# Norm rows stored unsplit, scaled rows in their own tiles, one gate product on another engine

## The chip, the cores and the metric

The kernel runs on one core of a Trainium2 chip. The metric is the time of one execution on the device in microseconds (us), the median of several runs. In the profile PE is TensorE (PEld its weight loads), DVE is VectorE, ACT is ScalarE, POOL is GpSimd and SP is SyncE, which here issues nearly all DMAs.

## The reference, cut to what matters

One layer of a diffusion backbone over 2048 latent tokens of width 1024 with a context of 256 tokens, all in float32. Two groups of heads (a gated recurrence in both directions and a spatial gating unit, "sgu") read one input projection. Around the change it computes:

```python
o_mlp = chunk_sgu(...)                       # gelu(u) * (W_s LN(gelu(v)) + b), per head and 128 positions
o = concatenate([o_hg, o_mlp], axis=-1)
x = x + g1 * (o @ w_out[l])                  # output projection, 1024 x 1024
h2 = modulate(rmsnorm(x, norm_ffn[l]), sh2, sc2)
...
a, g = split(h2 @ w_up[l], 2)                # up-projection, 1024 x 5632
x = x + g2 * ((a * gelu(conv3x3(g) + conv_b)) @ w_down[l])
return rmsnorm(x, norm_final)
```

## The kernel before

**Products.** A float32 matrix is used as a sum of two rounded parts, high and low: a copy on ScalarE rounds the high part, a subtraction gives the low part (`split`, lines 135 to 140). A product of two such pairs is three matmul passes (high by high, high by low, low by high). The output projection and the up-projection each multiply 2 x 2 blocks with seven block products in place of eight (Strassen's scheme in Winograd's form). The seven right-hand operands live in seven pairs of tiles `B[i]`, `B[i][0]` the high part, `B[i][1]` the low; `products` issues a product of 12 matmuls of 512 columns, on weights `Ah`, `Al`. `Unit.prep` makes these from `raw` rows: per product a cast on ScalarE and a subtraction on GpSimd (L140), and for four of the seven products a sum on GpSimd (L1247 to L1253). It runs three products ahead (`LOOK`). Products 2, 3, 5 and 6 add onto a bank of PSUM (`ux`, `uz`) that must first be read by the addition of an earlier product, on VectorE (L1378 in the output projection).

**Stages in order.** (1) The projection with the heads. The last head's sgu makes, for each of two 512-column parts (`n0` = 0 and 512), a layernorm (`ln`), four spatial matmuls and a scaling (`mix`, L717), and a product with gelu(u) on GpSimd (`both`, L685), whose result is stored to `oT_d`. At four banks before the end `open_wo` frees the heads' tiles and queues `load`, which fetches the first rows of `oT_d` and splits the first two operands of `w_out`. (2) The output projection: eight pairs of row tiles (`pairs`, n = 0 to 7), seven products each in the order 0, 1, 2, 4, 3, 6, 5 (`SEVEN`). Rows of x are fetched by `fetch_x` (L1350), the products added to them (L1378), the result stored to `xn_d` (L1388). (3) With it, the second norm, one pair behind: sum of squares on ScalarE (L1389), the root on GpSimd (`rstd`), scaling of the rows in place (L1300), then four steps `k` of four transposes each on PE (L1303), two activations that modulate (L1315) and three differences that make the seven operands (L1318 to L1320). The steps start a set stretch of modelled PE time after the pair's last product (`how`: 10.0, then every 2.6). For the first half (n = 0 to 3) they're stored as they are in `yd[0]` (L1322); for the second (n = 4 to 7) they are split into high and low, and both are stored in `yd[1]` (L1326, L1327). (4) The up-projection, first half then second: during pair 7 the first half's operands are loaded from `yd[0]` on ScalarE's DMA queue (L1391) and split in `B` (`in_place`). After an operand's last use in the first half its two parts for the second are loaded from `yd[1]` (`load_b`, L1409). Then the down-projection.

**What sets the order.** Each engine works through its own queue in order. A scheduler places instructions of a queue by a model of their readiness, except that those under `pin` keep their order in the program; `tc.issue_after(i)` puts what is inside it behind instruction `i` of its engine. Work at the side is queued in two pumps (`hg_q`, `bg_q`) and let in between matmuls by modelled PE time. DMAs issued by SP also go in the order of its queue: one that waits holds up those behind it.

**Tiles around the change.** `px` holds `cv` (3 tiles, rows of x), `fl` (2, the norm's seven operands), `yst` (2, their high part); `pv`, opened at block 4 in place of `po`, holds `v` (3, rows of x). `po` holds the first rows of the projection (`first0`, `first1`), two pairs of weights and a sum for row tile 0.

Of the kernel before, what the change touches and what calls it, by code (L numbers as in the profile page):

```python
# [9 lines left out]
F32 = mybir.dt.float32  # L10
# [8 lines left out]
P = 128  # L19
# [69 lines left out]
def tile_trunk(ctx, tc, x, c, cx, c_ctx, w_ada, b_ada, norm_mix, norm_ffn, w_in, hg_norm, sgu_g, sgu_b,  # L89
# [107 lines left out]
    with es1:  # L197
# [480 lines left out]
        def sgu(hh, h):  # L678
# [3 lines left out]
            def both(n0):  # L682
                if n0 in z and n0 in u:
                    zt = z.pop(n0)
                    G.tensor_mul(zt, zt, u.pop(n0))  # L685
                    st(oT_d[hh][:, 4 + h, n0:n0 + 512], zt)
# [6 lines left out]
            def sv(n0, n, pj):  # L693
# [3 lines left out]
                def ln():  # L697
# [217 lines left out]

        def in_place(i):
            split(B[i][0], B[i][1], B[i][1].bitcast(F32), V, pin)

# [218 lines left out]
        def open_wo():  # L1137
# [5 lines left out]
            po = eso.enter_context(tc.tile_pool(name="po", bufs=1, side="right", reuse_waits="tile"))  # L1143

            def load():
                ahead.extend(po.tile([P, 4, 2 * P], F32, name=f"first{k}") for k in range(2))
                ahead.extend(tuple(po.tile([P, 4, P], F32R, name=f"A{w}{i}", align_bytes=AL) for w in "hl") for i in range(2))
                ahead.append(po.tile([P, 4, P], F32, name="s2"))
                four = pw.tile([P, 4, 4, 512], F32R, name="four", align_bytes=AL)
                for n, (i, w) in enumerate(((1, 0), (2, 1), (2, 0), (4, 1))):  # L1150
                    B[i][w] = four[:, n]
# [122 lines left out]
    yd = [dr.tile([P, 2, 7, 4, 512], F32, name=f"yd{hh}") for hh in range(2)]  # L1274

# [17 lines left out]
    with ExitStack() as esv:  # L1293
        def second_norm(hh, g0, xs, ss, bank_, first, step):

            r = rstd(px, ss, 2, 1.0 / D)

            def scale():
                for i in range(2):
                    scaled.append(pin(V.tensor_scalar(out=xs[i], in0=xs[i], scalar1=r[:, i:i + 1], scalar2=None,  # L1300
                                                      op0=ALU.mult)))
            yield scale
            yield first  # L1303
            cl = slice(g0 // 2 * P, g0 // 2 * P + P)
            for k in range(4):
                pt = bank_()
                for kk in range(2):
                    for i in range(2):
                        o = kk * 256 + i * P
                        T.transpose(pt[:, o:o + P], xs[i][:, (k + 4 * kk) * P:(k + 4 * kk + 1) * P], ident)  # L1310
# [9 lines left out]
                V.tensor_sub(fl[:, 6, :], fl[:, 1, :], fl[:, 2, :])  # L1320
# [13 lines left out]
        def prep_o(m):  # L1334
# [8 lines left out]
            elif n == NCH - 1 and i in (6, 5):  # L1343
                units[1].load_half(6 - i)

        def fetch_x(n):
            out = []
            for i in range(2):
                t = v_tile()[:, :D] if i or n in (0, NCH - 1) else pv.tile([P, D], F32, tag="v", name="v", bufs=3)
                ld(t, x[(2 * n + i) * P:(2 * n + i + 1) * P, :])  # L1350
                out.append(t)
                if n == 0:
                    wo_raw((3, 6)[i])
            return out

        xts = {0: fetch_x(0)}
        wo_raw(5)
        pairs[1].load()
        in_place(4)
        with tc.issue_after(rooted[-1].ins):  # L1360
            for m in range(LOOK):
                prep_o(m)
        todo = {2: lambda: in_place(3), 3: lambda: in_place(6), 4: lambda: in_place(5)}
        later, scales = {}, {}
        for m, (u, i) in enumerate(blocks):
            n = pairs.index(u)
            if i == 0:
                u.x, xs = xbank(), xts.pop(n)
                ss = px.tile([P, 2], F32, tag="ss", name="ss", bufs=2)
                if 0 < n < NCH - 1:  # L1370
                    xts[n + 1] = fetch_x(n + 1)
            elif i == 4:
# [9 lines left out]
            prep_o(m + LOOK)  # L1382
            if m == 4:
                eso.close()
                pv = esv.enter_context(tc.tile_pool(name="pv", bufs=1, side="right", reuse_waits="tile"))
                xts[1] = fetch_x(1)
            if i in (6, 5):
                st(xn_d[2 * n + c], xs[c])  # L1388
                S.activation(dbank().rearrange("p a b -> p (a b)"), xs[c], AF.Square, accum_out=ss[:, c:c + 1])  # L1389
            if n == NCH - 1:  # L1390
                todo[m + 1] = lambda i=i: S.dma_start(B[i][1].bitcast(F32), yd[0][:, 0, i])  # L1391
                later[m + 4] = lambda i=i: in_place(i)
            if i == 5:
                how = (10.0, 2.6) if n + 1 < NCH else (10.0, 4.5)
                norm = second_norm(u.hh, u.f, xs, ss, lambda: dbank()[:, 0, :], *how)
                bg_q.drain()
# [9 lines left out]
    pf = esx.enter_context(tc.tile_pool(name="pf", bufs=1, reuse_waits="tile"))  # L1406

    def load_b(hh, i, w):
        ld(B[i][w].bitcast(F32), yd[hh][:, w, i])  # L1409

# [176 lines left out]
    for n, (u, i) in enumerate(prods):  # L1587
# [14 lines left out]
        if n == 12:  # L1602
            edges = px.tile([P, 7, P], F32R, tag="yst", name="edges", bufs=2).bitcast(F32)
            edges = edges[:, :4, :].rearrange("p f (w c) -> p f w c", w=2)
        with tc.issue_after(scaled[-1].ins) if n < 8 else nullcontext():
# [280 lines left out]
```

## Time and profile before

| | us |
|---|---|
| median of 3 runs | 2431.0 |
| lowest, highest | 2428.29, 2431.53 |
| the profiled execution | 2425.86 |
| its span, first to last instruction | 2423.8 |

The profiled execution has a mean granted TensorE clock of 0.988. Where rows of the profile are shown, a line of the timeline has the start, the duration, the engine, the line of the kernel, the operation, what it writes and reads, its shape and how many of them were merged; what stands in brackets is how long the engine was idle before it, and what ended that. A line of waits has the engine that waited, for whom, the sum in us, the number of times and the longest. A line of groups has the number of instructions, then busy us and mean ns of one, then the idle time before them.

The larger costs by name: `pj` is the input projection, `ux` and `uz` are the banks of the seven-product stages, `dn` is used by the norm's transposes, the convolution and the down-projection.

### The profile page before, as it was taken

What the parts mean: (1) busy time and instruction counts of PE and PEld (TensorE: products, weight loads), DVE (VectorE), ACT (ScalarE), POOL (GpSimd) and SP (SyncE); (2) the same over time, 40 slices, a digit from 0 to 9 for tenths busy, and PEclk for the clock granted to TensorE, in tenths of its full rate; (3) what the DMA queues carried; (4) which work ended last, traced back from release to release, by engine and by line L of the source; (5) the groups of instructions that cost most, each with busy time, mean ns of one, the idle gap of its engine ahead of it and who ended that gap; (6) DMA issues with size and microseconds to landing.
All of it is one profiled execution on the core that took longest, in us unless ns stands there. A gap on an engine that the chain in (4) does not pass through costs nothing.

```text
span 2423.8 us, 37053 instructions
## 1 busy us (share of the span) xinstructions
PE 2338.8 (96%) x14059; PEld 1923.4 (79%) x14059; DVE 1666.0 (69%) x2158; ACT 1058.3 (44%) x1820; POOL 1011.8 (42%) x875
## 2 busy tenths in 40 slices
PE   7999999999999998996899999999999999999998
PEld 6887878877887876775788888888888887888887
DVE  4767687576667666776896666549777763776876
ACT  3554443444455444445544444344444443332243
POOL 0022121111112327764887878878788860000002
PEclk8999999999999998998999999999999999999999
DMA  8465455664444226669322232642222238834645
GB/s 309 125 202 163 160 157 187 232 208 138 160 149 131 101 76 234 219 231 296 107 94 82 91 97 78 239 178 97 93 87 92 84 125 336 306 118 152 229 149 200
DMA packets 300695, 394.63 MB, mean 163 GB/s; under 512 B 32581, under 2 KB 219229, under 8 KB 296933
## 3 DMA queue, kind: packets, MB, share of 16 engines
q1 hardware_dynamic: 296220, 384.17, 47.0%
q10 hardware_dynamic: 4297, 8.10, 1.1%
q8 instruction: 110, 1.80, 0.3%
q14 instruction: 68, 0.56, 0.1%
HBM read 284.13 MB, written 108.08 MB: 162 GB/s over the span
## 4 chain that ended last, share of the span: by engine, by line
PE 46%; issue 2%; DMA 2%; POOL 1%; DVE 1%; ACT 0%; SPq 0%; POOLq 0%; DVEq 0%; ACTq 0%
PE ux L70 19%; PE uz L70 14%; PE dn L70 13%; DMA sT<-wd 1%; POOL rr L1746 1%; DMA sS<-m 0%; DMA mr<-m 0%; DMA yd<-yst 0%; DVE rest L140 0%; ACT four L139 0%; POOL raw L1251 0%; POOL ra L1745 0%; SPq L1671 0%; POOL Al L140 0%; POOL ra L1743 0%
## 5 line engine op out<-in xcount | busy, mean ns | idle before, releaser
L1453 DVE SCALAR_TENSOR_TENSOR dn<-gp,taps,dn 128x1024 f32<-128x1024 f32 x352 | 448.2, 1284 | 99.6 <-ACT dn L1450 95.0
L140 POOL TENSOR_TENSOR Al<-raw,Ah 128x512 fp32r<-128x512 f32 x306 | 404.7, 1338 | 100.0 <-ACT Ah L139 55.9
L70 PE MATMUL dn<-thl,mhl 128*128 128x512 f32 x1680 | 383.6, 390 | 3.4 <-ACT thl L139 3.2
L70 PEld LDWEIGHTS dn<-thl,mhl 128*128 128x128 f32 x1680 | 316.0, 188 | 70.9 <-ACT thl L139 4.1
L70 PE MATMUL pj<-xh,whi 128*128 128x512 f32 x896 | 366.4, 409 | 0.0
L70 PE MATMUL pj<-xl,whi 128*128 128x512 f32 x896 | 351.6, 393 | 0.0
L70 PE MATMUL pj<-xh,wlo 128*128 128x512 f32 x896 | 350.6, 392 | 0.0
L139 ACT CAST Ah<-raw 128x512 fp32r<-128x512 f32 x306 | 188.6, 619 | 270.9 <-PE ux L70 145.8
L70 PE MATMUL ux<-rest,Ah 128*128 128x512 f32 x832 | 209.8, 395 | 3.6 <-ACT wo L139 3.6
L70 PEld LDWEIGHTS pj<-xh,whi 128*128 128x128 f32 x896 | 168.3, 188 | 38.9 <-issue 7.2
L70 PEld LDWEIGHTS pj<-xh,wlo 128*128 128x128 f32 x896 | 168.3, 188 | 35.8
L70 PEld LDWEIGHTS pj<-xl,whi 128*128 128x128 f32 x896 | 168.7, 188 | 29.5 <-DVE xl L259 0.6
L70 PEld LDWEIGHTS ux<-rest,Ah 128*128 128x128 f32 x832 | 158.7, 191 | 38.3 <-ACT wo L139 4.0
L70 PE MATMUL uz<-rest,Ah 128*128 128x512 f32 x624 | 184.3, 390 | 0.5 <-DVE cv L1378 0.5
L591 POOL TENSOR_TENSOR K<-K,tot 128x512 f32<-128x512 f32 x40 | 62.8, 1571 | 256.0 <-DVE K L591 95.6
L70 PE MATMUL uz<-four,Ah 128*128 128x512 f32 x416 | 162.2, 390 | 0.0
L1743 POOL TENSOR_SCALAR ra<-ss 128x1 f32<-128x1 f32 x8 | 3.2, 397 | 365.6 <-ACT jk L1734 365.6
L140 DVE TENSOR_TENSOR wlo<-raw,whi 128x1024 fp32r<-128x1024 f32 x68 | 83.5, 1229 | 96.9 <-ACT whi L139 94.3
L70 PEld LDWEIGHTS uz<-rest,Ah 128*128 128x128 f32 x624 | 117.1, 188 | 25.3 <-DVE cv L1378 0.8
L139 ACT CAST whi<-raw 128x1024 fp32r<-128x1024 f32 x68 | 71.3, 1048 | 133.4 <-PE pj L70 101.0
L70 PE MATMUL uz<-rest,Al 128*128 128x512 f32 x416 | 116.7, 397 | 6.2 <-POOL Al L140 6.2
L1247 POOL TENSOR_TENSOR raw<-raw 128x512 f32<-128x512 f32 x51 | 66.6, 1305 | 117.9 <-DMA raw<-in_w_up_dram 80.8
(345 smaller groups left out, 4493.6 us busy)
## 6 DMA issues: line engine op xcount, KB each, us to landing
raw<-in_w_up_dram SPq DMA_DIRECT2D x88, 512.0 KB, 3.5
mr<-m SPq DMA_DIRECT2D x85, 512.0 KB, 5.3
raw<-in_w_in_dram SPq DMA_DIRECT2D x68, 512.0 KB, 4.1
sT<-wd SPq DMA_DIRECT2D x88, 256.0 KB, 5.6
raw<-in_w_ada_dram SPq DMA_DIRECT2D x32, 512.0 KB, 3.5
yd<-fl SPq DMA_DIRECT2D x32, 448.0 KB, 3.4
m<-cv SPq DMA_DIRECT2D x22, 544.0 KB, 2.7
raw<-in_w_down_dram SPq DMA_DIRECT2D x22, 512.0 KB, 3.6
```

The costliest lines, as they stand in the source:

```text
L70: return self.engine.matmul(out, lhsT, rhs, **kw)
L139: keep(S.copy(hi, raw))
L140: (eng or G).tensor_sub(lo, raw, hi.bitcast(F32))
L591: e.tensor_mul(view(K2, row * W + o, src), view(K, o, src), view(tot, t0, [[4, n], [ts, 2], [0, B]]))
L1247: G.tensor_sub(a21, a11, a21)
L1453: V.scalar_tensor_tensor(out=cr, in0=gt[:, t // 3:t // 3 + RH, t % 3:t % 3 + GW], scalar=taps[:, t * NF + f:t * NF + f + 1], in1=cr, op0=A ...
L1743: G.tensor_scalar(out=a, in0=ss, scalar1=plus, scalar2=None, op0=ALU.add)
L1746: G.tensor_tensor(out=r, in0=a, in1=mhalf[:, :1], op=ALU.pow)
```

## The change

Five parts:

- **Scaled rows in own tiles.** L1300 no longer scales the rows in place but into a new tile `sc` (2 in `px`, in the place of `yst`), from which the transposes read.
- **Rows stored raw.** The second norm stores its seven operands unsplit for both halves; `yd[hh]` has one copy. In pairs 1 to 6 they're made in `yf` (3 tiles in `pv`), in pairs 0 and 7 in `fl` as before.
- **Split when fetched.** For the second half, an operand's rows are loaded three products after its last use in the first half and split in place four products after that.
- **The last gate's product** (second half, last head, `n0` = 512) is on VectorE. The splits of operands 0 and 1 of `w_out` move from `load` to behind the two `mix` of that head; those of the others (`todo`) come one product apart from product 0 on.
- **Fetches and tiles.** The first 128 rows of x are fetched in `open_wo`'s `load`; later rows at product 4 of the pair before (of `SEVEN`, the fourth place), into `v` (2 tiles) and `cv`. `pv` opens at block 10. `in_place` keeps the copy's order and, where asked, the subtraction's. The norm's steps start at 9.0 and come every 2.8.

```diff
 def both(n0):
-    G.tensor_mul(zt, zt, u.pop(n0))
+    (V if (hh, h, n0) == (1, NH - 1, 512) else G).tensor_mul(zt, zt, u.pop(n0))
...
     z[n0] = nt
     both(n0)
+    if (hh, h) == (1, NH - 1):
+        in_place(n0 // 512, pin)
...
-def in_place(i):
-    split(B[i][0], B[i][1], B[i][1].bitcast(F32), V, pin)
+def in_place(i, keep=lambda i: i):
+    raw = B[i][1].bitcast(F32)
+    pin(S.copy(B[i][0], raw))
+    keep(V.tensor_sub(B[i][1], raw, B[i][0].bitcast(F32)))
...
 def load():
...
-    in_place(0)
-    yield 5.0
-    in_place(1)
+    ld(ahead[5], x[:P, :])
     yield 0.0
...
 def scale():
     for i in range(2):
-        scaled.append(pin(V.tensor_scalar(out=xs[i], in0=xs[i], scalar1=r[:, i:i + 1], ...
+        sc.append(px.tile([P, D], F32, tag="sc", name="sc", bufs=2))
+        scaled.append(pin(V.tensor_scalar(out=sc[i], in0=xs[i], scalar1=r[:, i:i + 1], ...
...
-    yf = c_tile()
-    fl = yf.bitcast(F32)
+    fl = (pv[0].tile([P, NK, P], F32, tag="yf", name="yf", bufs=3) if 0 < n < NCH - 1 else
+          c_tile().bitcast(F32))
...
-    if hh == 0:
-        st(yd[0][:, 0, :, k, cl], fl[:, :7, :])
-    else:
-        hi = px.tile([P, 7, P], F32R, tag="yst", name="yst", bufs=2)
-        split(hi, yf[:, :7, :], fl[:, :7, :], V)
-        st(yd[1][:, 0, :, k, cl], hi.bitcast(F32))
-        st(yd[1][:, 1, :, k, cl], fl[:, :7, :])
+    st(yd[n // 4][:, :, k, cl], fl[:, :7, :])
...
 def fetch_x(n):
-        t = v_tile()[:, :D] if i or n in (0, NCH - 1) else pv.tile([P, D], F32, tag="v", name="v", bufs=3)
+        t = (pv[0].tile([P, D], F32, tag="v", name="v", bufs=2) if i == 0 and 1 < n < NCH - 1 else
+             v_tile()[:, :D])
...
-todo = {2: lambda: in_place(3), 3: lambda: in_place(6), 4: lambda: in_place(5)}
+todo = {0: lambda: in_place(4), 1: lambda: in_place(3), 2: lambda: in_place(6), 3: lambda: in_place(5)}
...
-    if m == 4:
+    if m == 10:
         eso.close()
...
+    if i == 4 and n < NCH - 1:
+        xts[n + 1] = fetch_x(n + 1)
...
-    how = (10.0, 2.6) if n + 1 < NCH else (10.0, 4.5)
+    how = (9.0, 2.8) if n + 1 < NCH else (10.0, 4.5)
...
 for j in range(7):
-    if last_use[j] == n - 4:
-        for w in range(2):
-            load_b(1, j, w)
+    if last_use[j] == n - 3:
+        ld(B[j][1].bitcast(F32), yd[1][:, j])
+    elif last_use[j] == n - 7:
+        in_place(j)
```

More of the change, by code (lines that the diff above doesn't have):

```diff
@@ L1143, in open_wo @@
             po = eso.enter_context(tc.tile_pool(name="po", bufs=1, side="right", reuse_waits="tile"))
-            def load():
[L1146 to L1151, printed above, removed]
+            four = pw.tile([P, 4, 4, 512], F32R, name="four", align_bytes=AL)
+            for n, (i, w) in enumerate(((1, 0), (2, 1), (2, 0), (4, 1))):
+                B[i][w] = four[:, n]
+            ahead.extend(po.tile([P, 4, 2 * P], F32, name=f"first{k}") for k in range(2))
+            pairs_a = po.tile([P, 4, 4, P], F32R, name="pairs_a", align_bytes=AL // 2)
+            ahead.extend((pairs_a[:, 2 * i], pairs_a[:, 2 * i + 1]) for i in range(2))
+            ahead.append(po.tile([P, 4, P], F32, name="s2"))
+            ahead.append(po.tile([P, D], F32, name="x0"))
+            def load():
                 for k in range(2):
@@ L1273, in tile_trunk @@
             raw_at[n] = lambda u=units[m], k=i // 6: u.load_half(k)
-    yd = [dr.tile([P, 2, 7, 4, 512], F32, name=f"yd{hh}") for hh in range(2)]
+    yd = [dr.tile([P, 7, 4, 512], F32, name=f"yd{hh}") for hh in range(2)]
     def prep(n):
@@ L1293, in tile_trunk, with second_norm @@
     with ExitStack() as esv:
-        def second_norm(hh, g0, xs, ss, bank_, first, step):
+        def second_norm(n, xs, ss, bank_, first, step):
             r = rstd(px, ss, 2, 1.0 / D)
+            sc = []
             def scale():
                 for i in range(2):
-                    scaled.append(pin(V.tensor_scalar(out=xs[i], in0=xs[i], scalar1=r[:, i:i + 1], scalar2=None,
+                    sc.append(px.tile([P, D], F32, tag="sc", name="sc", bufs=2))
+                    scaled.append(pin(V.tensor_scalar(out=sc[i], in0=xs[i], scalar1=r[:, i:i + 1], scalar2=None,
                                                       op0=ALU.mult)))
@@ L1303, in second_norm @@
             yield first
-            cl = slice(g0 // 2 * P, g0 // 2 * P + P)
+            cl = slice(n % 4 * P, n % 4 * P + P)
             for k in range(4):
@@ L1309, in second_norm @@
                         o = kk * 256 + i * P
-                        T.transpose(pt[:, o:o + P], xs[i][:, (k + 4 * kk) * P:(k + 4 * kk + 1) * P], ident)
-                yf = c_tile()
-                fl = yf.bitcast(F32)
+                        T.transpose(pt[:, o:o + P], sc[i][:, (k + 4 * kk) * P:(k + 4 * kk + 1) * P], ident)
+                fl = (pv[0].tile([P, NK, P], F32, tag="yf", name="yf", bufs=3) if 0 < n < NCH - 1 else
+                      c_tile().bitcast(F32))
                 for kk, dims in ((0, [[7 * P, 2], [1, P]]), (1, [[4 * P, 2], [1, P]])):
@@ L1344, in prep_o @@
                 units[1].load_half(6 - i)
+        pv = []
         def fetch_x(n):
@@ L1348, in fetch_x @@
             for i in range(2):
-                t = v_tile()[:, :D] if i or n in (0, NCH - 1) else pv.tile([P, D], F32, tag="v", name="v", bufs=3)
+                t = (pv[0].tile([P, D], F32, tag="v", name="v", bufs=2) if i == 0 and 1 < n < NCH - 1 else
+                     v_tile()[:, :D])
                 ld(t, x[(2 * n + i) * P:(2 * n + i + 1) * P, :])
                 out.append(t)
-                if n == 0:
-                    wo_raw((3, 6)[i])
-            return out
-        xts = {0: fetch_x(0)}
-        wo_raw(5)
+            return out
+        wo_raw(3)
+        xts = {0: [ahead[5], v_tile()[:, :D]]}
+        ld(xts[0][1], x[P:2 * P, :])
+        for i in (6, 5):
+            wo_raw(i)
         pairs[1].load()
-        in_place(4)
         with tc.issue_after(rooted[-1].ins):
@@ L1382, in tile_trunk @@
             prep_o(m + LOOK)
-            if m == 4:
+            if m == 10:
                 eso.close()
-                pv = esv.enter_context(tc.tile_pool(name="pv", bufs=1, side="right", reuse_waits="tile"))
-                xts[1] = fetch_x(1)
+                pv.append(esv.enter_context(tc.tile_pool(name="pv", bufs=1, side="right", reuse_waits="tile")))
+            if i == 4 and n < NCH - 1:
+                xts[n + 1] = fetch_x(n + 1)
             if i in (6, 5):
@@ L1390, in tile_trunk @@
             if n == NCH - 1:
-                todo[m + 1] = lambda i=i: S.dma_start(B[i][1].bitcast(F32), yd[0][:, 0, i])
+                todo[m + 1] = lambda i=i: S.dma_start(B[i][1].bitcast(F32), yd[0][:, i])
                 later[m + 4] = lambda i=i: in_place(i)
             if i == 5:
-                how = (10.0, 2.6) if n + 1 < NCH else (10.0, 4.5)
-                norm = second_norm(u.hh, u.f, xs, ss, lambda: dbank()[:, 0, :], *how)
+                how = (9.0, 2.8) if n + 1 < NCH else (10.0, 4.5)
+                norm = second_norm(n, xs, ss, lambda: dbank()[:, 0, :], *how)
                 bg_q.drain()
@@ L1406, in tile_trunk @@
     pf = esx.enter_context(tc.tile_pool(name="pf", bufs=1, reuse_waits="tile"))
-    def load_b(hh, i, w):
-        ld(B[i][w].bitcast(F32), yd[hh][:, w, i])
     RW = GW + 2
@@ L1602, in tile_trunk @@
         if n == 12:
-            edges = px.tile([P, 7, P], F32R, tag="yst", name="edges", bufs=2).bitcast(F32)
-            edges = edges[:, :4, :].rearrange("p f (w c) -> p f w c", w=2)
+            edges = px.tile([P, D], F32, tag="sc", name="edges", bufs=2)[:, :4 * P]
+            edges = edges.rearrange("p (f w c) -> p f w c", f=4, w=2)
         with tc.issue_after(scaled[-1].ins) if n < 8 else nullcontext():
```

2 lines of the change are left out of this document (removed).

## The prediction

> **What bounds the kernel now.** I read the page first: the share of each engine, then the forty slices of the span.
>
> ```profile
> PE 2338.8 (96%) x14059; PEld 1923.4 (79%) x14059; DVE 1666.0 (69%) x2158; ACT 1058.3 (44%) x1820; POOL 1011.8 (42%) x875
> PE   7999999999999998996899999999999999999998
> PEclk8999999999999998998999999999999999999999
> ```
>
> TensorE (PE) is the bound. No edit here takes a matmul away, so all that can be won is time in which PE waits or runs slowly. The slices show where that lies: a slice is 60.6 us, and the dips at slices 16 to 20 are 909 to 1212 us, the output projection with the second norm and the start of the up-projection. So I cut that stretch at the starts of products and read the windows (columns: length, busy us of PE, PEld, DVE, ACT, POOL, granted clock, DMA share, GB/s); the last row is the seam between the halves of the up-projection.
>
> ```profile
> 923.34:955.72 32.38, 25.01 (x86) 18.98 (x86) 19.76 (x12) 12.24 (x15) 26.05 (x17) 0.79 0.63 235
> 955.72:976.68 20.96, 20.96 (x101) 17.33 (x100) 14.76 (x17) 9.63 (x19) 18.47 (x16) 1.00 0.51 168
> 976.68:1096.28 119.60, 109.25 (x502) 87.33 (x500) 87.13 (x111) 56.70 (x102) 78.69 (x66) 0.99 0.69 225
> 1096.28:1131.99 35.71, 25.17 (x98) 19.47 (x96) 22.17 (x28) 12.98 (x21) 12.60 (x9) 0.86 1.00 319
> 1131.99:1190.30 58.31, 44.59 (x190) 35.51 (x188) 44.87 (x44) 36.44 (x50) 42.69 (x25) 0.91 0.61 189
> 1535.00:1595.00 60.00, 60.00 (x266) 49.67 (x266) 22.74 (x25) 23.80 (x41) 49.11 (x42) 1.00 0.88 338
> ...
> 1179.58 5.44 PE ux L70 x24
> ```
>
> The last line, from the chain of waits, prices the work: 24 matmuls in 5.44 us, 0.2267 each, so a product of 12 takes 2.72 and a pair of row tiles (7 products) 19.04. Pair 1 (955.72 to 976.68) also carries a norm's 16 transposes and loses nothing: 20.96, so 16 transposes cost 1.92. Against that:
> - pair 0: 32.38 - 19.04 = **13.3** lost
> - pairs 2 to 6: 119.60 - 5 x 20.96 = **14.8**
> - pair 7: 35.71 - 20.96 = **14.8**
> - the first 14 up-projection products with a norm: 58.31 - 38.09 - 1.92 = **18.3**
>
> Together 61.2 us: the ceiling of this change, with some 2.6 just before pair 0 (below). The seam loses nothing now, so there the change can only cost. What PE waits for, from 895 to 1190 us:
>
> ```profile
> PE dn L74 <- DVE v L1300: 11.6, 6, 6.3
> PE ux L70 <- ACT four L139: 6.7, 1, 6.7
> PE ux L70 <- POOL Al L140: 6.6, 2, 4.0
> PE uz L70 <- POOL Al L140: 6.2, 1, 6.2
> PE dn L74 <- ACT fl L1315: 3.7, 2, 2.1
> PE ux L70 <- ACT wo L139: 3.6, 1, 3.6
> PE mi L70 <- DVE nt L709: 2.6, 2, 2.0
> ```
>
> **Scaled rows in own tiles.** The transposes wait for L1300, which scales the rows in place. The waits of VectorE (DVE) say why it is late:
>
> ```profile
> DVE v L1300 <- DMA xn<-v: 24.1, 5, 7.5
> ```
>
> The unscaled rows are being stored to `xn`, and the scaling must not overwrite them until the store has read them. Five times, 24.1 us, during which everything behind L1300 on DVE stands. A tile of its own ends that wait; the instruction count is the same. Next late is the root on POOL, then DVE's queue. The fetch of x moves from product 0 to product 4 of a pair and now takes the `v` tile of two pairs ago, so on SyncE's queue it waits for that pair's `xn` store: the wait moves from DVE to SP, where loads of the next `raw` and the norm's stores stand behind it. They have some 11 us (four products) to spare, and the longest wait above is 7.5, so I cost it at 0; uncovered it costs up to 7.5 a pair in pairs 4 to 7.
>
> **Rows stored raw.** For pairs 4 to 7 the norm now also splits its rows and stores two copies.
>
> ```profile
> L140 DVE TENSOR_TENSOR fl<-fl,yst 128x896 fp32r<-128x896 f32 x16 | 21.2, 1324 | 10.4 <-ACT yst L139 10.4
> L139 ACT CAST yst<-fl 128x896 fp32r<-128x896 f32 x16 | 15.1, 941 | 30.4 <-issue 21.3 <-DVE fl L1320 9.0
> yd<-yst SPq DMA_DIRECT2D x16, 448.0 KB, 3.9
> ```
>
> Gone: 21.2 us of DVE plus 10.4 it idled for the cast, 15.1 of ScalarE (ACT), 16 stores of 448 KB (7.3 MB). None of it is PE's, but it delays PE through DVE's order. At the seam of the two stages:
>
> ```profile
> 1140.16 1.09 DVE L140 TENSOR_TENSOR fl<-fl,yst 128x896 fp32r<-128x896 f32 x1 [0.68 <-ACT yst L139]
> 1141.17 0.68 DVE L1378 TENSOR_TENSOR cv<-ux,cv 128x512 f32<-128x512 f32 x1
> 1142.00 3.57 PE L70 MATMUL ux<-wo,Ah 128*128 128x512 f32 x8 [6.69 <-ACT four L139]
> ```
>
> The page blames ACT for the 6.69, but the `ux` bank is freed by the add at 1141.17, which stood behind the norm's split. With three `yf` buffers in place of two, the 3.7 us of waits for `fl` (a buffer held by a store) should go too. I take: pairs 2 to 6 lose 2 instead of 14.8 (**-12.8**); pair 7 loses 1.4 instead of 14.8 (**-13.4**), as the DVE wait of 6.3 and the 3.6 both lie there with a slow clock behind each (0.86).
>
> At the start of the up-projection the seven operands of the first half are split as before, and Al on POOL stays the limit (6.6 us of waits). Each split collides with it:
>
> ```profile
> 908.74 2.28 DVE L140 TENSOR_TENSOR wo<-wo 128x2048 fp32r<-128x2048 f32 x1
> 927.44 3.37 DVE L140 TENSOR_TENSOR four<-four,rest 128x2048 fp32r<-128x2048 f32 x1
> 931.92 1.29 POOL L1253 TENSOR_TENSOR first<-first,s 128x512 f32<-128x512 f32 x1
> 928.75 3.21 POOL L1251 TENSOR_TENSOR first<-s,first 128x512 f32<-128x512 f32 x1
> ```
>
> A subtraction takes 2.28 alone and 3.37 beside POOL; POOL's operation 3.21 instead of 1.29. So a collision costs POOL 1.9 us. The first nine products need 9 Al and 8 sums: 17 x 1.29 = 21.9 us; seven collisions add 13.4: 35.3 against 9 x 2.72 = 24.5 plus a lead of three products (8.2): 2.6 late, and the norm of pair 7 adds scalings and a root. I leave 8 of 18.3 (**-10.3**), between 0 and the 15 that all collisions in a row would give.
>
> **Last gate's product on DVE, row tile 0 fetched early.** POOL's part of the seam before pair 0:
>
> ```profile
> 922.14 1.54 PE L70 MATMUL mi<-wsT,nt 128*128 128x128 f32 x8 [1.99 <-DVE nt L709]
> 933.16 1.27 POOL L685 TENSOR_TENSOR nt<-nt,gu 128x512 f32<-128x512 f32 x1
> 934.46 0.32 SPq L686 DMA_DIRECT2D oT<-nt  x1
> 935.30 0.91 SPq L1350 DMA_DIRECT2D cv<-in_x_dram  x2
> 941.46 0.69 DVE L1378 TENSOR_TENSOR cv<-ux,cv 128x512 f32<-128x512 f32 x1 [3.63 <-DMA cv<-in_x_dram]
> ```
>
> The product ran at 933.16, behind POOL's sums; its store held SP's queue until 934.46, so x left at 935.30, and the first add, which frees `ux`, ran at 941.46. On DVE the product comes soon after the mix (which ends at 923.7), at the 0.69 us of a 512-wide add; POOL saves 1.27, and x is there before pair 0's first add. The splits of operands 0 and 1 (908.74 above is the first's subtraction) move to behind the two mixes: that frees DVE for `nt` (the mix waited 1.99 and 0.66: I take **-1.5**), and puts two more splits (2 x 2.28 to 3.37) into the crowded stretch. There one product needs one split and one add on DVE, 2.97 to 4.06 us against PE's 2.72: six of them lose 1.5 to 8. I leave 5.3 of 13.3 (**-8**).
>
> **Fetch and split at the seam.** Each operand is now loaded once (1 MB, not 2) three products after its last use and split four later; first use is 11 or 12 after the last. Added: seven copies on ACT and seven subtractions on DVE, both idle there (ACT 23.80, DVE 22.74 of 60). POOL isn't:
>
> ```profile
> 1584.05 5.03 POOL L140 TENSOR_TENSOR Al<-raw,Ah 128x512 fp32r<-128x512 f32 x4
> 1590.45 1.30 POOL L140 TENSOR_TENSOR Al<-raw,Ah 128x512 fp32r<-128x512 f32 x1 [1.36 <-PE ux L70]
> ```
>
> It works without a gap up to 1589.08 and only then waits for PE again. Collisions (1.9 each, seven at most 13.4) fall into that; I count three that aren't covered, less about 2 us of lead: **+4**, from 0 to 13.
>
> Of the clock: the trace has a short wait behind which PE ran slowly.
>
> ```profile
> 1068.79 0.33 PE L74 MATMUL dn<-ident,v 128*128 128x128 f32 x1 [2.11 <-ACT fl L1315]
> 1069.98 3.49 PE L70 MATMUL ux<-wo,Ah 128*128 128x512 f32 x8
> ```
>
> After an idle 2.11 us, eight matmuls took 3.49, not 8 x 0.2267 = 1.81; so I count a wait with the slow work behind it. The Trainium skill ("TensorE: Matmul & The Clock Gate", What's actually happening) states that the clock falls only after an idle window of about 3.4 us. By that rule this wait would return only itself, and the -12.8 would be 1.7 smaller; this trace differs from it.
>
> **The sum.** -12.8 - 13.4 - 10.3 - 1.5 - 8 + 4 = -42.0 us. The profiled execution took 2425.9 us (2423.8 span and 2.1 around it), which gives 2383.9. The median of the runs, 2431.0, lies 5.1 above it, and I forecast for that: **2389 us** (2379 to 2399).
>
> **The rivals.**
> - **The scaling is still late**, because DVE itself is behind, so the change doesn't do what it says. For it: the transposes come 1 us earlier than before (9.0 instead of 10.0), and L1300 has DVE work before it. Against: 21.2 + 10.4 us leave DVE. Price: the 11.6 us of the first PE wait stays: 2401. Chance 0.12.
> - **POOL and DVE collide everywhere**: pair 0 wins 3, pairs 2 to 7 23 in all, the up-projection's start 3, the seam loses 11: -18, 2413. For it: 3.21 instead of 1.29. Against: the DVE work removed collides too. Chance 0.20, a small part of it with the SP wait on top and no change.
> - **All is hidden**: -61 - 2.6 and nothing at the seam: 2367. For it: pair 1 shows a full pair without loss. Against: POOL's count above. Chance 0.15.
> - **Splits on PE's path, slower.** Nine splits stand in new places: two behind the mixes, seven at the seam. One that PE must wait out costs the copy, 1.91, and the subtraction, 3.2: 5.1, and some 1.5 of slow clock; nine of them 59, against gains of 46: +13, 2444. It decides when the rows land later than some 17 us after the load's issue (three products to spare before the split, two after). Against: a 1 MB `yd` load took 8.5. Chance 0.05.
>
> ```profile
> L139 ACT CAST rest<-rest 128x2048 fp32r<-128x2048 f32 x6 | 11.4, 1906 | 7.8 <-DMA rest<-wo_d 7.8
> wo<-yd ACTq DMA_DIRECT2D x2, 1024.0 KB, 8.5
> ```
>
> For the second rival stand the rows above, 3.21 and 3.37 where the two engines meet. The Trainium skill ("SBUF — State Buffer", Who interferes with whom) states that a VectorE operation with two SBUF inputs and a GpSimd one that reads SBUF block each other whole, by order of issue. By that rule each added split would cost POOL up to its full 2.28, 2.5 us more over seven; the trace agrees to within that.
>
> **How the numbers follow.** Forecast 0.48, the rivals 0.12, 0.20, 0.15 and 0.05. A measurement tells about 0.2%, 5 us, from no change. Faster by more: all but the slower rival and 0.03 of the collisions: 0.92; same 0.03; slower 0.05. The range takes the forecast, the late scaling, most of the collisions and half of the last case: 2370 to 2418.
>
> **What would show it.** Right: no wait of L1300 for `xn`, pairs 2 to 7 near 21 us each, the product of the gate before 926 us, no `yst`, 7.3 MB less written. Wrong: a pair still over 22.5 with DVE named, SP waiting at L1350 with POOL waiting for `raw`, or PE idle between 1500 and 1600 us, for Al (collisions) or for an operand (splits late).

## The result, and the profile after

The changed kernel takes **2412.08 us** (median of 4 runs, 2410.57 to 2413.37) against 2429.64 for the kernel before in the same session: a ratio of 0.993, 95% interval 0.9913 to 0.9947. It is faster by 17.6 us, where 42 were forecast; the second rival (collisions everywhere, 2413) has the time.

First the page, the busy time of each engine and the slices of the span and of the clock:

```profile
PE 2337.6 (97%) x14059; PEld 1920.6 (80%) x14059; DVE 1675.3 (70%) x2150; ACT 1055.7 (44%) x1811; POOL 1025.9 (43%) x874
PE   7999999999999998997999999999999999999998
PEclk8999999999999999998999999999999999999999
```

The norm's splits (21.2 us) left DVE, seven splits and the gate's product (some 17 us at 2.28 and 0.9) came, and it is 9.3 us busier (1675.3 against 1666.0): operations on it got longer. The same windows as before, cut at the starts of products (columns: length, busy us of PE, PEld, DVE, ACT, POOL, granted clock, DMA share, GB/s). They are pair 0, pair 1, pairs 2 to 6, pair 7, the first 14 products of the up-projection, and the 14 products of the seam:

```profile
922.28:952.24 29.96, 23.31 (x89) 17.86 (x88) 22.67 (x14) 12.06 (x13) 29.80 (x15) 0.83 0.68 253
952.24:973.90 21.66, 20.31 (x95) 16.52 (x94) 14.76 (x15) 8.54 (x16) 19.32 (x17) 1.00 0.50 169
973.90:1083.79 109.89, 106.49 (x502) 86.31 (x501) 86.34 (x106) 52.12 (x98) 77.78 (x66) 1.00 0.67 223
1083.79:1112.24 28.45, 24.51 (x102) 19.29 (x101) 18.84 (x25) 12.12 (x20) 12.34 (x10) 0.89 0.97 331
1112.24:1165.18 52.94, 44.81 (x190) 35.26 (x188) 41.28 (x43) 31.00 (x44) 41.11 (x26) 0.93 0.49 157
1545.98:1594.36 48.38, 41.70 (x170) 32.22 (x168) 23.68 (x20) 22.77 (x30) 40.32 (x25) 0.96 0.35 121
```

Pairs 2 to 6 lose 109.89 - 104.80 = 5.1 us now instead of 14.8, pair 7 7.5 instead of 14.8, the up-projection's start 52.94 - 40.0 = 12.9 instead of 18.3. Pair 0 has hardly moved, and POOL is busy in it without a gap (29.80 of 29.96). The seam, which lost nothing, loses 48.38 - 38.08 = 10.3.

What PE waits for from 915 to 1170 us, and below it the longest wait of VectorE from 950 to 1112 us:

```profile
PE ux L70 <- ACT Ah L139: 6.5, 2, 5.6
PE ux L70 <- POOL Al L140: 5.3, 3, 4.0
PE ux L70 <- DVE cv L1380: 4.3, 3, 2.0
PE dn L74 <- DVE sc L1307: 1.4, 1, 1.4
```

```profile
DVE yf L1325 <- ACT yf L1322: 22.2, 12, 2.2
```

The wait of 24.1 us for the `xn` stores is gone, and PE's wait for the scaled rows went from 11.6 us to 1.4. The longest that are left are one named ScalarE (5.6) and one for `Al` on POOL (4.0; for `Al` 5.3 in all, where there were 12.8).

### The profile page after: what moved, and what is told of

It is laid out like the page before. It is cut to its first block, busy times and chain, and to the rows that moved or that the text cites. A ratio compares the mean times of both kernels' runs of the same rounds, so it can differ in the third digit from the quotient of the medians.

```text
span 2409.0 us, 36962 instructions
## 1 busy us (share of the span) xinstructions
PE 2337.6 (97%) x14059; PEld 1920.6 (80%) x14059; DVE 1675.3 (70%) x2150; ACT 1055.7 (44%) x1811; POOL 1025.9 (43%) x874
## 4 chain that ended last, share of the span: by engine, by line
PE 48%; issue 3%; DVE 2%; DMA 2%; POOL 2%; ACT 1%; SPq 0%; POOLq 0%; ACTq 0%; DVEq 0%
PE ux L70 20%; PE uz L70 15%; PE dn L70 13%; DMA sT<-wd 1%; POOL Al L140 1%; DVE yf L1325 1%; DVE yf L1326 1%; POOL rr L1747 0%; DMA mr<-m 0%; DMA sS<-m 0%; PE dn L74 0%; ACT yf L1322 0%; DVE cv L1380 0%; ACT rest L920 0%; POOL fl L1254 0%
## 5 line engine op out<-in xcount | busy, mean ns | idle before, releaser
L140 POOL TENSOR_TENSOR Al<-raw,Ah 128x512 fp32r<-128x512 f32 x306 | 412.4, 1362 | 80.7 <-ACT Ah L139 47.8
L70 PE MATMUL ux<-four,Ah 128*128 128x512 f32 x416 | 108.2, 403 | 13.5 <-ACT Ah L139 6.5
```

Of the source, the lines that this page charges most:

```text
L70: return self.engine.matmul(out, lhsT, rhs, **kw)
L140: (eng or G).tensor_sub(lo, raw, hi.bitcast(F32))
```

## The experiments

All times were taken beside the kernel before on the same chip (its medians 2429.5 to 2430.7). Where the experiments tell the stretches apart, this table is used: us lost, which is the time from the start of the first product to the start of the one after the last, less 2.72 a product and 1.92 where a norm's transposes lie. Pairs 0 and 1 are one column.

```
                           pairs 0,1  pairs 2-6  pair 7  up, first 14  seam   median
before                        13.3       14.8     14.8       18.3        0    2429.64
changed                       11.6        5.1      7.5       12.9      10.3   2412.08
e1  no subtractions            2.7        5.9      3.5       11.8        0    2386.59
e2  seam unsplit              11.7        7.3      5.3       14.6        0    2404.35
e3  scaled in place           11.6       23.9      6.1       16.6      11.7   2436.49
e4  gate product on POOL      16.2        4.3      7.8       12.8      12.1   2413.99
e5  last yf tile in fl        11.7        5.1      4.7       12.0       8.8   2409.20
e6  seam from PSUM            11.6        5.4      7.7       12.7       1.5   2403.78
e7  e5, e6, pair 0            9.2        4.4      5.3       11.4       1.9   2399.72
e8  e1 and e5                  2.9        6.0      5.2        3.5        0    2382.54
e9  all splits from PSUM      10.9        4.2      5.5       17.6       1.5   2402.55
e10 in place, x early         11.6       13.6      8.0       15.5      10.0   2421.55
e11 every second split         7.5        5.0      4.7       12.0       2.0   2396.75
e12 e11 and two of the start   7.5        5.1      6.2       11.5       1.6   2394.33
```

The start of pair 0, before which these kernels are nearly the same, lies between 918.9 and 927.5 us in the profiled executions, so a single span is good to some 4 us only. The row of e4 is of an execution of 2421.44 us, 7.5 above its median.

### Collisions or lateness: e1, e2

The theory was that a split's subtraction on VectorE and POOL's operations hold each other up; the rival, that the split comes late (copy, load, POOL's own amount).

```diff
 def in_place(i, keep=lambda i: i):
...
     pin(S.copy(B[i][0], raw))
-    keep(V.tensor_sub(B[i][1], raw, B[i][0].bitcast(F32)))
```

> The subtraction of every operand split (line 921, 21 of them: seven output operands, seven of the first half, seven of the second) is left out, so the low part of these operands stays the raw row; the copies, the loads and everything on POOL stay. Collisions (a VectorE subtraction and a POOL operation keep each other waiting): POOL's operations beside the seven splits of pair 0, of pair 7 with the start of the up-projection, and of the seam fall from 3.2 or 3.3 us to 1.3, the losses fall from 10.5 to about 3 (pair 0), from 12.9 to about 6 (up-projection's start) and from 9.7 to under 1.5 (seam): some 20 us, about 2392. Rival, lateness (the copies on ScalarE, the single load and POOL's own work are late, the subtraction is not): POOL's operations may get shorter, but the seam still loses over 5 and the whole is within 8 us of the changed kernel, 2404 or more.

Measured: 2386.59 us, ratio 0.9816 (0.9803 to 0.9829). Two rows of POOL's timeline in pair 0, of the changed kernel and then of this run:

```profile
928.13 3.20 POOL L1256 TENSOR_TENSOR first<-s,first 128x512 f32<-128x512 f32 x1
931.29 3.33 POOL L1258 TENSOR_TENSOR first<-first,s 128x512 f32<-128x512 f32 x1
```

```profile
919.41 1.31 POOL L1257 TENSOR_TENSOR first<-first,s 128x512 f32<-128x512 f32 x1
922.38 1.29 POOL L1255 TENSOR_TENSOR first<-s,first 128x512 f32<-128x512 f32 x1
```

With the copies and loads still there, the 3.2 us fall to 1.3, pair 0's loss all but goes and the seam's goes wholly. That carries the theory for these two places. (In pair 0 VectorE had been busy for 22.67 of the 29.96 us and POOL for all of them; here POOL is busy for 13.73 of 20.73.) Pair 7 loses 3.5 instead of 7.5 here, but 5.2 in e8, which has no subtractions either, and 4.7 in e5, which has them: nothing follows for it. The theory fails at the start of the up-projection, which loses 11.8 instead of 12.9 where about 6 was expected.

```diff
-if last_use[j] == n - 3:
-    ld(B[j][1].bitcast(F32), yd[1][:, j])
-elif last_use[j] == n - 7:
-    in_place(j)
+if last_use[j] == n - 4:
+    for w in range(2):
+        ld(B[j][w].bitcast(F32), yd[1][:, j])
```

> At the seam of the halves nothing is split: both parts of each operand are loaded from the raw rows, two loads where the kernel before had them, so that both parts are raw rows; the rest is the changed kernel. If the seam's split costs what the trace says, 9.7 us, the time is about 2402, the stretch from 1560 to 1620 us loses nothing, and no load of raw there takes 18 us. Rival: POOL was late there anyway (it was busy without a gap before), and the new order of the norm brought the loss: 2408 or more.

Measured: 2404.35 us, 0.9887 (0.9874 to 0.9901). The seam loses nothing, so its 10.3 us belong to the split, and the norm's new order has no part in them. The whole moved by 7.7 and not by the 9.7 that were expected, which is within the scatter of the stretches ahead (pairs 2 to 6 and the start lose 3.9 more in this execution, pair 7 2.2 less).

### One operand from PSUM: e6

If the conflict is about two operations that read two operands each from SBUF, it should end when the subtraction reads one of them from PSUM, with as many elements on VectorE as before.

```diff
+def by_bank(i):
+    raw = B[i][1].bitcast(F32)
+    pin(S.copy(B[i][0], raw))
+    for h in (slice(0, 2), slice(2, 4)):
+        t = dbank()
+        pin(S.copy(t, raw[:, h, :]))
+        V.tensor_sub(B[i][1][:, h, :], t, B[i][0][:, h, :].bitcast(F32))
...
 elif last_use[j] == n - 7:
-    in_place(j)
+    by_bank(j)
```

> The seven splits at the seam of the halves subtract from a copy of the raw rows in PSUM (two banks each time, made by ScalarE), so that VectorE's subtraction has one operand in PSUM and one in SBUF; as many elements on VectorE as before, 1.9 us more on ScalarE per operand. Theory, collisions of two operations that both read two operands from SBUF: POOL's operations from 1545 to 1590 us fall to 1.3 us each, the 10.3 us lost there fall under 2, and the time is 8 to 10 us lower, about 2403. Rival, any VectorE work beside POOL (or the splits' lateness) is the cause: POOL's operations stay near 3 us there, the loss stays over 7, or it grows, since ScalarE has more to do.

Measured: 2403.78 us, 0.9897 (0.9881 to 0.9913). POOL and VectorE in the seam, first in the changed kernel:

```profile
1563.37 9.51 POOL L140 TENSOR_TENSOR Al<-raw,Ah 128x512 fp32r<-128x512 f32 x3 [1.79 <-ACT Ah L139]
...
1581.03 1.26 POOL L1252 TENSOR_TENSOR raw<-raw 128x512 f32<-128x512 f32 x1 [3.63 <-DMA raw<-in_w_up_dram]
```

```profile
1566.14 2.29 DVE L921 TENSOR_TENSOR four<-four,rest 128x2048 fp32r<-128x2048 f32 x1 [0.18 <-ACT rest L920]
...
1569.24 5.79 DVE L921 TENSOR_TENSOR rest<-rest 128x2048 fp32r<-128x2048 f32 x2 [0.21 <-ACT rest L920]
```

and then in this run:

```profile
1555.37 1.30 POOL L1264 TENSOR_TENSOR raw<-fl,raw 128x512 f32<-128x512 f32 x1
1556.63 1.30 POOL L1266 TENSOR_TENSOR raw<-raw,fl 128x512 f32<-128x512 f32 x1
```

```profile
1555.90 2.36 DVE L929 TENSOR_TENSOR rest<-dn,rest 128x1024 fp32r<-128x1024 f32 x2 [0.76 <-ACT dn L928]
```

Before, three `Al` beside four subtractions took 3.17 us each; here two subtractions of together 2.36 us lie over POOL's operations, and those keep their 1.30. The seam loses 1.5 instead of 10.3. So it's not VectorE's work beside POOL that costs, but the second operand in SBUF. The Trainium skill ("SBUF — State Buffer", Who interferes with whom) says that a VectorE instruction with at most one SBUF input, outside the modes that use two ports, doesn't contend with GpSimd; this agrees with it (1.30 beside 2.36). The row at 1581.03 stands where the changed kernel loses most: POOL waits 3.63 us for `raw` rows, and PE then waits 3.05 for `Al`. But POOL waits for `raw` in this run too, 2.38 and 3.70 us, and up to 3.6 in e1, and PE loses little or nothing by it. So it isn't shown that the collisions made those loads late; it fits that they had used up the lead that covers such a wait.

### The start of the up-projection: e5, e8

There e1 had failed. The timeline of the changed kernel, PE, ScalarE and SP's queue:

```profile
1127.57 3.78 PE L70 MATMUL ux<-four,Ah 128*128 128x512 f32 x8 [5.65 <-ACT Ah L139]
```

```profile
1126.41 0.58 ACT L1517 COPY keep<-ux 128x512 f32<-128x512 f32 x1 [4.87 <-DMA yd<-yf]
1126.89 0.62 ACT L139 CAST Ah<-s 128x512 fp32r<-128x512 f32 x1
```

```profile
1122.52 0.52 SPq L1328 DMA_DIRECT2D yd<-yf  x1
```

PE waits for a cast `Ah`; the cast stands behind the first copy into `keep`; and that copy waits for a store of the norm, issued at 1122.52. `keep` lies in the pool `pf`, which opens when `pv` closes and takes its room, and the change had put the norm's `yf` into `pv`. The wait was new, and the prediction hadn't seen it.

```diff
-... if 0 < n < NCH - 1 else
+... if 0 < n < NCH - 1 and (n, k) != (NCH - 2, 3) else
```

> Only the last tile of the norm of pair 6 (n = 6, k = 3) comes from the fl tiles instead of the yf buffers of the pool pv; everything else is the changed kernel. Theory: the first copy of the up-projection into keep waits for the last store of a yf buffer, because the pool pf is laid over the pool pv that the change gave the yf buffers to; PE stands 5.65 us for it and runs slowly behind it. Then the wait of PE for line 139 at the third product of the up-projection goes, its first seven products lose about 6 instead of 13.9 us, and the time falls by 6 to 8 us, to about 2405. Rival: the third product is late because of the collisions of POOL and VectorE at 1123 us or of ScalarE's queue; then the wait stays, named by another operation, and the time moves by under 2 us.

Measured: 2409.20 us, 0.9915 (0.9902 to 0.9928), which can't be told from the changed kernel. The copy into `keep` now runs at once, and a wait for POOL is behind it:

```profile
1118.72 0.59 ACT L1517 COPY keep<-ux 128x512 f32<-128x512 f32 x1
```

```profile
1126.88 0.50 PE L70 MATMUL ux<-four,Al 128*128 128x512 f32 x1 [3.07 <-POOL Al L140]
```

The wait was rightly named and wrongly priced: 6 to 8 us were expected, the stretch gave 0.9. In e1, where the collisions were gone, the same product waited longer for the same store:

```profile
1113.82 3.78 PE L70 MATMUL ux<-four,Ah 128*128 128x512 f32 x8 [8.28 <-ACT Ah L139]
```

So each cause may have been hidden behind the other. e8 takes both away: the edits of e1 and e5 in one kernel.

> The subtraction of every operand split is left out (the low part stays the raw row) and the last yf tile comes from the fl tiles: the two single runs in one. Theory: at the start of the up-projection two causes of about the same length lie side by side, the wait for the last store under keep and POOL's collisions with the splits, and each hides the other, so that taking either away brought only 1 us. Both away, the first fourteen products lose about 4 us (1.9 of them transposes) instead of 14.9 in the changed kernel, 13.7 without the subtractions and 13.9 with the last tile elsewhere, and the time is 9 to 10 us under the run without subtractions: about 2377. Rival: a third cause, late raw loads or the norm's root, holds the stretch: it still loses over 9 us and the time is within 4 us of that run, 2383 or more.

Measured: 2382.54 us, 0.9809 (0.9794 to 0.9824). The first 14 products take 43.49 us, against 52.94 (neither away), 51.79 (no subtractions) and 52.02 (last tile elsewhere): 1.1 and 0.9 alone, 9.5 together.

```profile
1096.70:1148.49 51.79, 43.51 (x189) 35.46 (x188) 26.50 (x38) 31.54 (x44) 33.78 (x28) 0.90 0.54 179
```

```profile
1100.60:1144.09 43.49, 40.92 (x189) 33.53 (x188) 26.65 (x36) 30.63 (x44) 32.44 (x27) 1.00 0.63 211
```

The first row is of e1, the second of e8. The median is 4.1 under that of e1, not 9 to 10, and the span of the profiled execution 2.2: of the 8.3 won here, 1.7 went in pair 7, 1.9 ahead of pair 0, which starts later, and 2.2 behind the last product of the up-projection. The time lies at the rival's bound, but the rival held that the stretch still loses over 9, and it loses 3.5.

### Own tiles for the scaled rows: e3, e10

```diff
-sc.append(px.tile([P, D], F32, tag="sc", name="sc", bufs=2))
+sc.append(xs[i])
```

> The scaled rows go back over the unscaled ones (no tiles of their own), everything else as in the changed kernel. If the tiles of their own bring most of what pairs 2 to 7 gained (17 us), the wait of the scaling for the xn store comes back with over 15 us on VectorE and the time rises by 8 to 14 us, 2420 to 2426. Rival: the norm's own split and its two stores were what held VectorE; then the wait may come back, but the time rises by under 4 us.

Measured: 2436.49 us, 1.0022 (1.0013 to 1.0031): slower than before, and beyond what was expected. The wait for the `xn` store isn't what came back (3.2 us, once); PE and VectorE wait for something else from 960 to 1130 us:

```profile
PE ux L70 <- DVE v L1380: 14.9, 5, 3.9
DVE v L1380 <- DMA v<-in_x_dram: 8.3, 4, 2.3
```

A tile scaled in place is in use until the transposes, and x is now fetched late, at product 4, into such a tile: the additions wait for x. This run mixes the two; e10 fetches at product 0 again, with three `v` tiles, and keeps the scaling in place.

```diff
-if i == 4 and n < NCH - 1:
+if i == (4 if n < 2 else 0) and n < NCH - 1:
```

> The scaled rows go back over the unscaled ones, as in the run before of that kind, but the rows of x are fetched at product 0 of a pair (product 4 up to pair 1) and have three v tiles, as in the kernel before; the raw storing, the three yf buffers and the rest stay changed. If the 24 us of that run were mainly the late fetch (a tile in use until the transposes, fetched into at product 4): the waits for x go, the wait of the scaling for the xn store returns with 10 us or more on VectorE, and the time is 2417 to 2424. If the scaling in place alone costs the 24 us: 2432 or more. If own tiles are worth nothing once the norm's split is gone: within 4 us of the changed kernel, 2416 or less.

Measured: 2421.55 us, 0.9969 (0.9958 to 0.9981). By the time, own tiles with the late fetch are worth 9.5 us against this run. By pairs 2 to 6 it is 8.5 us (118.43 against 109.89; before 119.60), but 5.5 of these lie in pair 2 alone, whose x this run still fetches at product 4: SP issues the first load of these rows at 977.56 us and not at 961.14 as in the changed kernel, VectorE waits 2.81 us for them, and PE 4.50 for the addition onto `v`. Only from pair 3 on does the run test what it was made for. The length of each pair, in us:

```
                 pair 2   pair 3   pair 4   pair 5   pair 6   pair 7
before            23.78    22.17    22.32    25.03    26.30    35.71
changed           22.79    21.72    21.71    21.68    21.99    28.45
e10 in place      28.27    22.62    22.61    22.93    22.00    28.96
```

In pairs 3 to 7 the changed kernel wins 16.0 us over the kernel before, and this run wins 12.4 of them without the tiles. So the larger part there comes with the rest of the change, of which the split that left the norm is the likely piece (no run puts it back), and the tiles are worth some 3.6, not much more than these stretches scatter (pairs 2 to 6 lose 4.3 to 7.3 with the same code, in the changed kernel, e2, e4 and e6). The mechanism named isn't confirmed either: the scaling waits 3.9 us once for `xn`, not 10 or more. What the run shows in its place is PE waiting 4.7 us for scaled rows, where the changed kernel has 1.4. The two `sc` tiles of 4 KB a partition stand where the two `yst` of 3.5 KB were, so the one part made room for the other.

### The gate's product: e4

```diff
-(V if (hh, h, n0) == (1, NH - 1, 512) else G).tensor_mul(...)
+G.tensor_mul(...)
```

> The last gate's product goes back to POOL, everything else as in the changed kernel. By the sum in the prediction POOL has 1.27 us more in a stretch where it is never idle: 1.3 to 2 us slower, 2413 to 2414. If its store still holds up a load of x that pair 0's adds wait for: 4 us or more. If POOL is not the limit of pair 0: no change within 1 us.

Measured: 2413.99 us, 0.993 (0.9917 to 0.9944). Its median is 1.9 us higher, as expected, but its interval is the changed kernel's: the two are not told apart, and what the move of this product is worth isn't shown.

### Towards a better version: e7, e9, e11, e12

e7 joins e5 and e6, and splits operands 4, 3, 6 and 5 of pair 0 by `by_bank`.

```diff
-todo = {0: lambda: in_place(4), 1: lambda: in_place(3), 2: lambda: in_place(6), 3: lambda: in_place(5)}
+todo = {0: lambda: by_bank(4), 1: lambda: by_bank(3), 2: lambda: by_bank(6), 3: lambda: by_bank(5)}
```

> Both changes of the two runs before together, and four of pair 0's splits (operands 4, 3, 6 and 5) also from PSUM. If the gains add up: seam -9, start of the up-projection -7, and in pair 0 four of the seven collisions fewer, -4: about 20 us under the changed kernel, 2392. If ScalarE becomes late in pair 0 with eight more copies of 1 us: pair 0 loses more than 10.5 us, and the whole is about 2398 or more.

Measured: 2399.72 us, 0.9873 (0.9858 to 0.9888), 12.4 under the changed kernel where 20 were hoped for. In pair 0 both kinds of split stand side by side, VectorE and then POOL:

```profile
931.44 3.38 DVE L921 TENSOR_TENSOR four<-four 128x2048 fp32r<-128x2048 f32 x1
...
936.07 2.36 DVE L929 TENSOR_TENSOR four<-dn,rest 128x1024 fp32r<-128x1024 f32 x2 [0.65 <-ACT dn L928]
```

```profile
932.74 3.21 POOL L1264 TENSOR_TENSOR first<-s,first 128x512 f32<-128x512 f32 x1
...
937.17 1.29 POOL L140 TENSOR_TENSOR Al<-s,Ah 128x512 fp32r<-128x512 f32 x1
```

But pair 0 still loses most of what it lost, and now POOL is the one that waits, 2.13 and 1.68 us for `Ah`: ScalarE has 1.90 + 1.95 + 0.62 = 4.5 us an operand, more than a product's 2.72, and works from 932.70 to 951.2 us without a gap. VectorE waits for its copies 1.26 us three times, with the additions that free PE's banks behind them.

e9 adds the first half's seven operands:

```diff
-later[m + 4] = lambda i=i: in_place(i)
+later[m + 4] = lambda i=i: by_bank(i)
```

> The kernel of the last run of the batch before (seam and four of pair 0's splits from PSUM, last yf tile from fl) with the seven splits of the first half's operands from PSUM as well. They share their PSUM tiles with the norms' transposes and the sums of squares. If the collisions are what is left at the start of the up-projection: its first fourteen products lose 6 instead of 13.3, pair 7 loses 2 to 3 less, and the time is 7 to 10 us lower, about 2391. If the transposes now wait for PSUM tiles that a split holds: PE waits for dn, pair 7 and the start lose as much as before or more, 2400 or over.

Measured: 2402.55 us, 0.9887 (0.9874 to 0.9901). The start loses 17.6, more than in any other run of the changed kernel:

```profile
PE ux L70 <- DVE gp L1422: 4.1, 1, 4.1
PE ux L70 <- ACT Ah L139: 3.8, 2, 3.7
PE dn L74 <- DVE rest L929: 3.1, 2, 2.1
```

The transposes wait for PSUM tiles, as feared (3.1), and two further waits come with it. Casts stand behind ScalarE's extra copies (3.7). And the wait of 4.1 that is named after L1422, the clearing of `gp`'s borders, is another one by VectorE's timeline: the clearing starts at 1118.52 us without waiting, right behind an addition that frees the bank (1117.87, 0.68 us long), and that addition stood behind a split (1115.59, 2.35 us) which had itself waited 1.04 for ScalarE's copy.

So e11 takes e7, sends only operands 3 and 5 of pair 0 through PSUM, and clears `gp` 2 and 3 later; e12 adds operands 3 and 5 of the first half (the last line of the diff).

```diff
-todo = {0: lambda: by_bank(4), 1: lambda: by_bank(3), 2: lambda: by_bank(6), 3: lambda: by_bank(5)}
+todo = {0: lambda: in_place(4), 1: lambda: by_bank(3), 2: lambda: in_place(6), 3: lambda: by_bank(5)}
...
-for i in range(4):
+for i in range(2):
     border(i)
+for i in (2, 3):
...
+    todo[6 + i] = lambda i=i: border(i)
...
+later[m + 4] = lambda i=i: (by_bank if i in (3, 5) else in_place)(i)
```

> The kernel with the seam and pair 0 from PSUM and the last yf tile from fl, with two edits: in pair 0 only every second split (operands 3 and 5) goes through PSUM, and the borders of gp tiles 2 and 3 are cleared at products 8 and 9 of the up-projection. In pair 0 four splits through PSUM made ScalarE the next limit (4.5 us an operand, products 2.72); if that holds, pair 0 loses 5 to 6.5 us instead of 7.7 and the whole is 2 to 3 us lower, 2397. If POOL's collisions weigh as much as ScalarE: pair 0 loses 7 to 9 and the time is 2399 to 2402.

Measured: 2396.75 us, 0.9865 (0.9846 to 0.9883), 3.0 under e7, which lies within the intervals. Pairs 0 and 1 lose 7.5 instead of 9.2, with POOL busy again for nearly all of pair 0 (26.43 of the 26.51 us from 921.49 on).

> The same, and two of the seven splits at the start of the up-projection (operands 3 and 5) from PSUM. If two collisions less are worth more than ScalarE's 1.95 us for each: the first fourteen products lose 9 to 11 us instead of 13 and the time is 2 to 4 us under the run beside it, about 2394. If the PSUM tiles are held up again as with all seven: 2399 or more.

Measured: 2394.33 us, 0.9861 (0.9846 to 0.9876). Its edge over e11 lies within the intervals, and the start loses 11.5 us against 12.0, where 9 to 11 were expected. Both beat the kernel before (by 33 and 35 us) and the changed one (by 15 and 18).

## Why the prediction was wrong in size

The direction and the places were right; the gains were too large and one loss too small. In the profiled executions, forecast and measured (negative is a gain): before pair 0 -1.5, **-1.1**; pairs 0 and 1 -8, **-1.7**; pairs 2 to 6 -12.8, **-9.7**; pair 7 -13.4, **-7.3**; the up-projection's start -10.3, **-5.4**; the seam +4, **+10.3**. Together -42.0, **-14.9**; the span went from 2423.8 to 2409.0, the medians fell 17.6. Of the 27.1 us between the two sums, pairs 0 and 1 have 6.3, the seam 6.3, pair 7 6.1, the start 4.9, pairs 2 to 6 3.1.

The step that failed is the price of the splits that run beside a busy POOL. The prediction had that price right for one split (1.9 us on POOL) and then counted VectorE's time in pair 0, three of seven splits at the seam, and too little at the start.

- **Pair 0** failed outright. "Six of them lose 1.5 to 8" counted VectorE's time per product (2.97 to 4.06 against 2.72), and not POOL's: with six of its sums and `Al` at 3.2 to 3.4 us instead of 1.3, POOL was full (29.80 of 29.96 us). PE's longest wait there is 3.98 us for `Al`; one of 1.99 is VectorE's, an addition behind a split. e1 takes away 8.9 us, e7 2.4 with ScalarE the next limit.
- **The seam** was mis-sized: three collisions uncovered, less 2 of lead, against 10.3. POOL had been shown at work there without a gap. All seven splits collide: POOL's stretched operations from 1531 to 1576 us are 13.4 us longer in sum (one of 3.26, two of 4.60 together, one of 3.36, three of 9.51 and one of 2.97, against 1.29 each), the most that the prediction allowed, and only some 3 of it are covered. The bound of 13 held it.
- **The up-projection's start** left 8 of 18.3 for the seven collisions. Without the wait for `keep` it still loses 12.0 (e5), so that count was too low by itself; POOL's root for the norm, which the prediction named without a number, is stretched there too (2.75 us, against 0.72 in e8). The change also laid a second limit beside it, `keep` waiting for the last `yf` store, by which it still loses 11.8 when the subtractions are gone (e1). The prediction counted the three `yf` tiles as a gain and didn't ask what is laid over their pool. It took both away to see either (e8).
- **Pair 7** was set at 1.4 lost and lost 7.5. Two waits of 2.0 us for L1380 are in it, additions that stood behind the norm's differences. Both sets of differences had waited 2.2 us for ScalarE's modulation; of one all three are then stretched beside POOL (rows at the end), of the other one. How they fall differs between kernels with the same code up to there, 5.3 to 7.8 (e2, e4, e6), and it is 3.5 and 5.2 without the splits' subtractions. Why the step was so far off was not settled further.
- **Scaled rows in own tiles** and **rows stored raw** had one sum for both in pairs 2 to 6, which came nearer than the other large ones. But the mechanism given for the tiles isn't borne out: the wait of 24.1 us for `xn` is gone, yet it is nearly gone with the scaling in place too (3.9 in e10), and pairs 3 to 7 won most of their gain there without the tiles. Three of the five pairs take 21.7 us, the others 22.8 and 22.0, where 21 was said; PE waits up to 0.6 us for the addition onto `v` in most of them. The moved fetch, costed at 0, is covered in the changed kernel, and isn't where the rows are scaled in place (e3, and pair 2 of e10).
- **The rivals.** "POOL and DVE collide everywhere" gave the total, and by stretch came nearer than the forecast: pair 0 wins 3 (2.4), pairs 2 to 7 23 (17.0), the start 3 (5.4), the seam loses 11 (10.3). That its total fits so well is in part luck: it has pairs 2 to 7 too high by 6.0, the start too low by 2.4, and no wait for `keep`. Its row, 3.21 and 3.37, stood in the prediction; what spoke against it ("the DVE work removed collides too") could hold only in pairs 4 to 7, where the norm had split. The split on PE's path (slower) didn't come about: in the seam PE waited only 0.3 us twice for a split operand.
- **Signs named ahead**: the product of the gate ran at 925.99 us, `yst` is gone, and HBM writes fell by 7.3 MB, all as said. Of the signs of being wrong, PE idled for `Al` from 1500 to 1600 us, that of collisions, and pair 7 stayed over 22.5 with VectorE named.

## What to carry to other kernels

Moving elementwise work to an idle engine isn't free when it reads two operands from SBUF beside a full GpSimd: count the second engine's work in the stretch, add to it what each such operation costs there (here 1.9 us for a subtraction of 2.28), and only then look for cover. Where one operand came from PSUM, the collision went (e6), at the price of copies on ScalarE, 1.95 us an operand, and ScalarE must have the room (e7). And when tiles move to another pool, ask what is laid over that pool next: its first user here waited 4.87 us for the last store out of the old tiles. And when two limits lie side by side, taking either away shows next to nothing (1.1 and 0.9 us, against 9.5 for both).

## What the runs showed of the hardware that was not expected

A subtraction with one operand in PSUM took 2.36 us in two parts, against 2.28 for one with both in SBUF and nothing on POOL beside it. It left POOL's 1.29 us as it was, where the SBUF form took up to 3.38 and POOL 3.3. Small operations pay as much: the norm's differences of 128 columns take 0.29 us alone and 1.27 beside POOL, so that a set of three grows from 1.0 to 3.9 us, with the addition that frees PE's bank behind it (changed kernel, VectorE):

```profile
1099.86 0.29 DVE L1326 TENSOR_TENSOR yf<-yf 128x128 f32<-128x128 f32 x1
1103.30 1.42 DVE L1325 TENSOR_TENSOR yf<-yf 128x256 f32<-128x256 f32 x1 [2.23 <-ACT yf L1322]
1104.75 1.27 DVE L1326 TENSOR_TENSOR yf<-yf 128x128 f32<-128x128 f32 x1
1106.06 1.24 DVE L1327 TENSOR_TENSOR yf<-yf 128x128 f32<-128x128 f32 x1
1107.22 0.68 DVE L1380 TENSOR_TENSOR cv<-ux,cv 128x512 f32<-128x512 f32 x1
```
